# A layer of recurrent heads and pooling on one core: TensorE's side products in one block per slot, the solver's stores on another queue

## The chip, the cores and the metric

The kernel runs on one core of one Trainium2 chip, in one launch. The metric is the device time of an execution in microseconds; the time of a kernel is the median over its runs.

## What is computed

One layer of a decoder: a norm, one input projection of 3200 columns, two kinds of heads that share it, gates, one output projection, the residual and a last norm. There is one prompt of 2048 rows, and eight sequences of four rows each that go on from a given state (the sample).

```python
h = rmsnorm(x); p, g_rwkv, u, g_pool = split(h @ w_in)
ps = p + mu * (previous_row(p) - p);  r, k, v, xw, xa = split(ps)
decay = exp(-exp(-softplus(-(w0 + tanh(xw) @ w_decay)) - 0.5)); a = sigmoid(a0 + xa @ w_aaa)
kk = heads(k * k_k) / norm; k = k * (1 + (a - 1) * k_a)
for t in range(T):                          # per head, S is 64 x 64
    S = S * decay + (S @ -kk) x (kk * a) + v x k;  y[t] = S @ r
o_rwkv = (group_norm(y) + sum(r * k * r_k) * v) * silu(g_rwkv)
o_pool = (windowed_mean(u, 2|4|8|16) - u) @ pool_w * pool_scale * silu(g_pool)
out = rmsnorm(x + concat(o_rwkv, o_pool) @ w_out)
```

The new shift rows, the states S and the last rows of u are outputs too.

## The kernel before

The prompt is worked off in four groups of 512 rows. A group's input projection is 25 column blocks of 128: block 12 (the low-rank inputs) first, then six blocks for each of four pairs of heads: r, k, the pooling input, v, the pooling gate, the heads' gate. Weights and activations are split into a high and a low part of fp32r, so a block is eight **slots** of three matmuls (`pp`, lines 342 to 344: xh with wh, xl with wh, xh with wl), 512 columns wide. The last group also carries the sample and is cut into two runs of 272 columns; there a slot holds six matmuls. `proj` yields after each slot, and `run` (line 458) then calls `side` (line 446).

`side` steps the work that goes beside the projection, one step of each lane and in this order: the lane "solve", then every generator in `late`, then the lanes "prod", "fold" and "chain". What it issues on TensorE gets an edge to the slot's last projection matmul (`tc.issue_after(mark[0])`), so that it stands behind it in TensorE's order. A scheduler then lays out the order of each engine from these edges, the data's dependencies, the order in which the code traced the instructions, and its own model of when inputs are ready. TensorE, like each engine, works its queue off in that order. A pair is 48 slots long. Its side steps on TensorE are:

- `key_norms` (line 499): sums of squares per head (`sq`) eight slots behind the k projection, and the bonus sums (`bo`) six later. It stores the sums to dS in device memory, four small stores issued by ScalarE (line 510).
- `products` (line 572): after three yields, the pair products `pa` (line 585) from abd and bk, one of four blocks per slot. These are what VectorE and ScalarE make of k in `unit` (lines 529 to 548), with line 542 as the last. Then, once the pair before has ended its fold (`pend`), the products `pb` (lines 616 and 617) with two yields between.
- `solve` (line 625): stores the triangle Ab to dA (line 634, issued by ScalarE), loads it back as L in another layout through SP (line 639), waits six yields, and solves in 31 steps on POOL (lines 651 and 653). POOL masks three more tiles (lines 663 and 665), and after YQ = 16 yields TensorE turns the result (`xt`, line 673). Two products (`q1`, line 692, and `q2`, line 700, in one step) finish the inverse.
- `fold` (line 725): for four blocks, `z` (line 730), its copies into zbd, and `f` (line 738), to which VectorE adds the tile F (line 741). One yield lies between these steps.
- `pair_chain` (line 760): eight steps `ch` (line 771), two yields apart, each as soon as the fold has counted its chunk (`folded`). VectorE scales the state (line 773), ScalarE copies the output (line 775).
- `pair_back` (line 800): the group norm of the outputs on VectorE (last instruction line 798), five yields, then the transposes `try` (line 808).
- `values` (line 710, transposes `trv`), `pool_out` (`po`, line 859), `lora_out` (`z` of 512 columns, line 391).

```python
    def run(gen, every):
        for i, _ in enumerate(gen):
            side()
            step("x")
```

The products go into PSUM banks by tag: "pp" three, "mm" two, "pt" two, "ch" one. After the groups, the output projection (`out_tile`, line 1140, three matmuls per slot at lines 1157 to 1160) runs beside the last pairs and the sample. Weights are loaded by ScalarE's queue (lines 311 and 314), in the first group they are split on the way and kept in device memory through SP (line 323).

Of the kernel before, what the change touches and what calls it, by code (L numbers as in the profile page):

```python
# [2 lines left out]

# [13 lines left out]
P = 128  # L17
# [43 lines left out]
def tile_trunk(ctx, tc, xT, xtok, xsT, xstok, par, w_in, wlora, pool_w, w_out, norm_f, st_shift, st_wkv, st_pool,  # L61
               y_p, y_s, nsh_p, nwkv_p, npool_p, nsh_s, nwkv_s, npool_s):
    nc = tc.nc
# [237 lines left out]
    raws, wts, mark = {}, {}, {}  # L301
# [25 lines left out]
    def proj(g, m, xs):  # L327

        i = order.index((g, m))
        hi, lo = wts.pop(i)  # L330
        late_load = i + 2 < len(order) and order[i + 2][0]
        if not late_load:
            w_load(i + 2)
        last = g == NG - 1
        segs = []
        w = 272 if last else 512
        for s in range(2 if last else 1):
            pp = bank("pp", f"pp_{g}_{m}_{s}", 3) if i else bank("ch", "pp_first", 1)
            c = slice(s * w, (s + 1) * w)
            for kc in range(KC):  # L340
                xh, xl = xs[kc]
                PE.matmul(pp[:, :w], hi[:, kc, :], xh[:, c], start=(kc == 0), stop=False)  # L342
                PE.matmul(pp[:, :w], hi[:, kc, :], xl[:, c], start=False, stop=False)  # L343
                mark[0] = PE.matmul(pp[:, :w], lo[:, kc, :], xh[:, c], start=False, stop=(kc == KC - 1)).ins  # L344
                if s == 0 and kc == 2:
                    w_split(i + 1)
                    if late_load:
                        w_load(i + 2)
                if not last or kc % 2:
                    yield  # L350
            if g == 0 and m != 12:
                V.tensor_tensor(out=pp, in0=pp, in1=rb0[0], op=mult)
            if last:
                A.activation(spr[:, m, 16 * s:16 * s + 16], pp[:, 256:272], AF.Copy)
                segs.append((pp, 256 * s, 256))
            else:
                segs.append((pp, 0, G))
        return segs
# [44 lines left out]
            V.scalar_tensor_tensor(out=sg[:, a:a + n], in0=t1[:, a:a + n], scalar=1.0, in1=pp[:, :n], op0=add, op1=mult)  # L403
        return sg

    DH, DZ, DP, YQ = 6, 2, 4, 16

    def c3(ap):
        return ap.rearrange("p (c t) -> p c t", t=CH)
# [3 lines left out]
    rb0, low = [], []  # L413
    pend = [0]
    made = [None]
    chb = []
    lanes = {"prod": [], "solve": [], "fold": [], "chain": [], "x": [], "tail": []}
    late = []
# [23 lines left out]
    def drain(lane):  # L442
        while lanes[lane]:
            step(lane)

    def side():
        if not mark:
            return
        with tc.issue_after(mark[0]):
            step("solve")  # L450

            with tc.high_priority(0):
                step_late()
                step("prod")
                step("fold")
                step("chain")
# [42 lines left out]
    def key_norms(g, j, u, kk2, prod):  # L499

        nm = f"{g}_{j}"
        a = head_sums(kk2, f"sq_{nm}")
        for _ in range(DH + 2):
            yield
        sq = head_sums_mm(a, f"sq_{nm}")
        sqs = sb.tile([P, 512], F32, tag="tmp", name=f"sqs_{nm}", bufs=3)
        A.activation(sqs, sq, AF.Copy)
        for h in range(2):
            for b in range(2):
                nc.scalar.dma_start(u["dS"][b, h:h + 1],  # L510
                                    sqs[64 * h:64 * h + 1].rearrange("p (c b t) -> p b c t", b=2, t=32)[:, b])
        a = head_sums(prod, f"bo_{nm}")
        for _ in range(DH):
            yield
        bo = head_sums_mm(a, f"bo_{nm}")
        u["bv"] = sb.tile([P, 512], F32, tag="bv", name=f"bv_{nm}")
        A.activation(u["bv"], bo, AF.Copy)

    def unit(g, j, xs, nxs, lst, nst):
        nm = f"{g}_{j}"  # L520
        u = {}
        later((DZ if g else DZ + 7) if j == 0 else 1, decay(g, j, lst, u))
        r = shift(g, j, (yield from proj(g, j, xs)), "rps", 1)
        k = shift(g, 4 + j, (yield from proj(g, 4 + j, xs)), "kps", 1)
        while alive[0] >= 2 or lanes["prod"]:
            side()
        alive[0] += 1
        lam, cs, tha = u["lam"], u["cs"], u["tha"]
        kk2 = sb.tile([P, 512], F32, tag="tmp", name=f"kk2_{nm}", bufs=3)
        A.activation(kk2, k, AF.Square, scale=pr[:, KK + j:KK + j + 1])  # L530
        for h in range(2):
            q = slice(64 * h, 64 * h + 64)
            V.scalar_tensor_tensor(out=abd[q, :, q], in0=c3(k)[q], scalar=pr[q, KK + j:KK + j + 1],
                                   in1=lam[q, :, 0:CH], op0=mult, op1=mult)
        ab = sb.tile([P, 512], F32, tag="t1", name=f"ab_{nm}")
        A.activation(ab, tha, AF.Identity, scale=nkk[:, j:j + 1], bias=nkk[:, j:j + 1])
        V.tensor_tensor(out=cs, in0=k, in1=cs, op=mult)
        V.tensor_tensor(out=bk[:, :, 0:CH], in0=c3(cs), in1=c3(ab), op=mult)
        rd = sb.tile([P, NCH, CH], F32, tag="rd", name=f"rd_{nm}", bufs=1)
        V.tensor_tensor(out=rd, in0=c3(r), in1=lam[:, :, 1:], op=mult)  # L540
        A.activation(tha, tha, AF.Identity, scale=hka[:, j:j + 1], bias=oka[:, j:j + 1])
        V.tensor_tensor(out=bk[:, :, CH:2 * CH], in0=c3(cs), in1=c3(tha), op=mult)  # L542
        for h in range(2):
            q = slice(64 * h, 64 * h + 64)
            nc.sync.dma_start(rbd[q, :, h], rd[q])
        prod = sb.tile([P, 512], F32, tag="pd", name=f"prod_{nm}", bufs=1)
        V.scalar_tensor_tensor(out=c3(prod), in0=rd, scalar=pr[:, RK + j:RK + j + 1],
                               in1=bk[:, :, CH:2 * CH], op0=mult, op1=mult)
        dS = dr.tile([2, 2, NCH, 32], F32, tag="dS", name=f"dS_{nm}")
        u.update(rd=rd, dS=dS)  # L550
        lanes["prod"].append(products(g, j, u))
        kn = key_norms(g, j, u, kk2, prod)
        next(kn)
        late.append(kn)
        for m in SEQ[2:]:
            if m == 17:
                d = yield from pool_in(g, j, xs)
            elif m == 8:
                u["v"] = shift(g, 8 + j, (yield from proj(g, 8 + j, xs)), "kps", 1)
                later(8, values(g, j, u))  # L560
            elif m == 21:
                sg = gate(g, 21 + j, (yield from proj(g, 21 + j, xs)), "th0")
                later(DP, pool_out(g, j, d, sg))
            else:
                u["sg"] = gate(g, 13 + j, (yield from proj(g, 13 + j, xs)), "sg")
            if m == (SEQ[3] if SEQ[2] == 8 else 8):
                V.tensor_tensor(out=u["bv"], in0=u["bv"], in1=u["v"], op=mult)
            if m == SEQ[4] and j == NPAIR - 1 and g < NG - 1:
                drain("x")
                lanes["x"].append(prep_x(g + 1, nst, nxs, range(XB - KC, KC)))  # L570

    def products(g, j, u):

        nm = f"{g}_{j}"
        for _ in range(3):
            yield

        ka = sb.tile([P, NCH, P], F32, tag="ka", name=f"ka_{nm}")
# [30 lines left out]
        for b in range(4):  # L609
# [8 lines left out]
            A.activation(f, pb[64:128], AF.Copy)  # L618
            for h in range(2):
                A.activation(rb[64 * h:64 * h + 64, cr, :], pb[0:64, :, h, :], AF.Copy)  # L620
            yield
            yield
        u["made"] = True

    def solve(g, j, u):
# [5 lines left out]
        for h in range(2):  # L631
            for b in range(2):
                o = 64 * h + 32 * b
                nc.scalar.dma_start(dA[b, h].rearrange("c t i -> t c i"), Ab[o:o + 32, :, 32 * b:32 * b + 32])
        L = sb.tile([P, 32, 32], F32, tag="L", name=f"L_{nm}", bufs=1)
        a2 = sb.tile([P, 32], F32, tag="a2", name=f"a2_{nm}")
        for q in range(4):
            nc.sync.dma_start(a2[32 * q:32 * q + 32], dS.rearrange("b h c t -> (b h c) t"))
            nc.sync.dma_start(L[32 * q:32 * q + 32], dA.rearrange("b h c t i -> (b h c) t i"))
        for _ in range(6):  # L640
            yield
        V.tensor_scalar(out=a2, in0=a2, scalar1=L2_EPS, scalar2=None, op0=add)
        V.reciprocal(a2, a2)  # L643
# [39 lines left out]
        with tc.issue_after(made[0]):  # L683
            for h in range(2):
                o = 64 * h + 32
                V.transpose(T22[o:o + 32], tbd[o:o + 32, :, o:o + 32])
        yield
        q1 = [bank("mm", f"q1_{nm}_{h}", 2, (P, NCH, 32)) for h in range(2)]
        for c in range(NCH):
            for h in range(2):  # L690
# [2 lines left out]
        for h in range(2):  # L693
            o = 64 * h
            A.activation(qs[o:o + 32], q1[h][o:o + 32], AF.Copy)
        q2 = [bank("mm", f"q2_{nm}_{h}", 2, (P, NCH, 32)) for h in range(2)]
        for c in range(NCH):
            for h in range(2):
# [26 lines left out]
    def fold(g, j, u):  # L725

        def front(b):
            z = bank("pt", f"z_{g}_{j}_{b}", 2, (P, 2, P))
            for c in range(2):
                PE.matmul(z[:, c, :], tbd[:, 2 * b + c, :], u["rb"][:, 2 * b + c, :], start=True, stop=True)  # L730
            zb = zbd[b % 2]
# [9 lines left out]
            V.tensor_tensor(out=d, in0=f, in1=d, op=add)  # L741
            u["folded"] += 2

        yield
        front(0)
        for b in range(4):
            yield
            if b < 3:
                front(b + 1)
            yield  # L750
            back(b)
        pend[0] = 0
        yield

# [385 lines left out]
    def out_tile(o, res, dst, n, wo, nm):  # L1140
# [12 lines left out]
        for f in range(2):  # L1153
            pp = bank("pp", f"po_{nm}_{f}", 3)
            for c in range(8):
                wh, wl = wo[c, f]
                PE.matmul(pp[:m], hi[:, c, :m], wh, start=(c == 0), stop=False)  # L1157
                mark[0] = PE.matmul(pp[:m], hi[:, c, :m], wl, start=False, stop=(both and c == 7)).ins  # L1158
                if not both:
                    mark[0] = PE.matmul(pp[:n], lo[:, c, :n], wh, start=False, stop=(c == 7)).ins  # L1160
# [123 lines left out]
```

## Time and profile before

| | |
|---|---|
| Median of 3 runs | 1284.83 us (1283.09 to 1289.94) |
| Profiled execution, its own time | 1285.28 us |
| Its span, first to last instruction | 1283.6 us |
| Mean granted TensorE clock | 0.964 of full speed |
| Bytes moved | 200.18 MB, 156 GB/s in the mean |

The profile is one execution. Times are from the start of the span, engines are PE (TensorE matmul), PEld (its weight loads), DVE (VectorE), ACT (ScalarE), POOL (GpSimd) and SP; a name with q behind it is the engine's own instruction queue. A row of a timeline has the start, the duration, the engine, the line, the operation, out<-in by the program's names, shapes and count; in square brackets stands the idle time before it and who ended it. Matmuls overlap, so one matmul's cost to the next is the distance of their starts.

### The profile page before, as it was taken

Reading aid. Unit: us, or ns where it says so; the run is one execution under the profiler, and the core shown is the slowest. Engines: PE = TensorE matmul, PEld = TensorE weight load, DVE = VectorE, ACT = ScalarE, POOL = GpSimd, SP = SyncE. Lnnn points to the kernel's source line nnn. Section 1 sums busy time; section 2 is a strip of 40 time slices with the busy share of each in tenths; the row PEclk is TensorE's granted clock in tenths of the full one; section 3 lists DMA queues with packets and bytes.
Section 4 is the critical chain, followed back from the end, with each engine's and each line's share of the span. In section 5 each row is a group of like instructions: output and inputs, shape, how many; then the busy total and the mean of one; then the engine's idle time right before and its main releaser. Section 6 shows DMA issues by size and latency. Waiting matters only on the chain. (4 is left out here: it accounts for less than half of the span.)

```text
span 1283.6 us, 21090 instructions
## 1 busy us (share of the span) xinstructions
PE 1193.0 (93%) x7229; PEld 982.6 (77%) x7229; DVE 827.3 (64%) x2028; ACT 563.7 (44%) x1363; POOL 503.9 (39%) x1138
## 2 busy tenths in 40 slices
PE   5987989898989999999899899899999999999997
PEld 2766767676878787788688789898889877887685
DVE  5755685957565847766676667565656577745764
ACT  3454545444454544446353546353535453321112
POOL 5045446253252844727164708071808370000000
PEclk6988999999999999999999999999999899999999
DMA  7565655555565544547465546354444354433332
GB/s 246 178 219 177 206 186 178 180 173 156 158 193 164 169 139 152 185 134 200 135 186 160 148 129 188 125 153 138 132 136 136 115 155 155 144 109 99 125 110 69
DMA packets 153372, 200.18 MB, mean 156 GB/s; under 512 B 82480, under 2 KB 99120, under 8 KB 153264
## 3 DMA queue, kind: packets, MB, share of 16 engines
q1 hardware_dynamic: 109632, 104.90, 26.7%
q10 hardware_dynamic: 43632, 93.93, 23.2%
q8 instruction: 57, 0.93, 0.3%
q14 instruction: 51, 0.42, 0.1%
HBM read 139.39 MB, written 46.80 MB: 145 GB/s over the span
## 5 line engine op out<-in xcount | busy, mean ns | idle before, releaser
L342 PE MATMUL pp<-xh,wh 128*128 128x512 f32 (+1 forms) x992 | 367.6, 371 | 7.5 <-ACT xh L204 4.5
L343 PE MATMUL pp<-xl,wh 128*128 128x512 f32 (+1 forms) x992 | 364.7, 368 | 1.4 <-DVE xl L205 1.4
L344 PE MATMUL pp<-xh,wl 128*128 128x512 f32 (+1 forms) x992 | 363.1, 366 | 0.2 <-DVE wl L321 0.2
L342 PEld LDWEIGHTS pp<-xh,wh 128*128 128x128 f32 x992 | 189.9, 192 | 33.7 <-ACT xh L204 5.6
L343 PEld LDWEIGHTS pp<-xl,wh 128*128 128x128 f32 x992 | 189.8, 191 | 25.3 <-DVE xl L205 2.7
L344 PEld LDWEIGHTS pp<-xh,wl 128*128 128x128 f32 x992 | 189.5, 191 | 23.6 <-DVE wl L321 1.7
L651 POOL TENSOR_TENSOR Xt<-X,L 128x60 f32<-128x60 f32 (+24 forms) x496 | 191.9, 387 | 38.8
L653 POOL TENSOR_TENSOR X<-X,Xt 128x60 f32<-128x60 f32 (+24 forms) x496 | 179.8, 363 | 38.9
L646 POOL TENSOR_TENSOR X<-dmask,a 128x256 f32<-128x256 bf16 x16 | 10.8, 676 | 296.1 <-DVE a L643 281.3
L644 POOL TENSOR_TENSOR L<-L,a 128x1024 f32<-128x1024 f32 x16 | 31.1, 1947 | 164.7 <-DMA L<-dA 164.7
L771 PEld LDWEIGHTS ch<-SV,F 128*128 128x128 f32 x512 | 75.2, 191 | 19.7 <-ACT Y L775 8.7
L771 PE MATMUL ch<-SV,F 128*128 128x64 f32 x512 | 79.6, 266 | 3.1 <-ACT Y L775 1.8
L738 PE MATMUL f<-zbd,ka 128*128 128x256 f32 x256 | 68.4, 387 | 0.8 <-DVE zbd L733 0.5
L1157 PE MATMUL po_o<-woh,oh_o 128*128 128x512 f32 x160 | 67.4, 421 | 0.0
L773 DVE TENSOR_TENSOR SV<-ch,lc 64x128 f32<-64x128 f32 x112 | 33.0, 295 | 52.6 <-PE ch L771 47.1
L585 PE MATMUL pa<-bk,abd 128*128 128x192 f32 x256 | 56.2, 366 | 11.0 <-DVE bk L542 9.0
L1158 PE MATMUL po_o<-wol,oh_o 128*128 128x512 f32 x160 | 65.8, 411 | 0.0
L1160 PE MATMUL po_o<-woh,ol_o 128*128 128x512 f32 x160 | 65.1, 407 | 0.1
L733 DVE COPY zbd<-z 64x256 f32<-64x256 f32 x64 | 27.2, 427 | 55.8 <-ACT zbd L732 54.6
L775 ACT ACTIVATE Y<-ch 64x128 f32<-64x128 f32 x128 | 34.3, 268 | 64.3 <-DVE SV L773 56.3
L741 DVE TENSOR_TENSOR F<-f,F 128x512 f32<-128x512 f32 x64 | 44.1, 689 | 27.4 <-PE f L738 24.4
L585 PEld LDWEIGHTS pa<-bk,abd 128*128 128x128 f32 x256 | 49.7, 217 | 15.8 <-DVE bk L542 7.0
(447 smaller groups left out, 2332.7 us busy)
## 6 DMA issues: line engine op xcount, KB each, us to landing
wh<-wh ACTq DMA_DIRECT2D x75, 512.0 KB
wl<-wl ACTq DMA_DIRECT2D x75, 512.0 KB
wr<-in_w_in ACTq DMA_DIRECT2D x25, 512.0 KB
wh<-wh SPq DMA_DIRECT2D x25, 512.0 KB
wl<-wl SPq DMA_DIRECT2D x25, 512.0 KB
xr<-in_xT SPq DMA_DIRECT2D x32, 256.0 KB
L<-dA SPq DMA_DIRECT2D x64, 128.0 KB
oi<-o_d SPq DMA_DIRECT2D x16, 512.0 KB
```

The source lines that it names most:

```text
L342: PE.matmul(pp[:, :w], hi[:, kc, :], xh[:, c], start=(kc == 0), stop=False)
L343: PE.matmul(pp[:, :w], hi[:, kc, :], xl[:, c], start=False, stop=False)
L344: mark[0] = PE.matmul(pp[:, :w], lo[:, kc, :], xh[:, c], start=False, stop=(kc == KC - 1)).ins
L585: PE.matmul(pa[:, c, :], abd[:, 2 * b + c, :], bk[:, 2 * b + c, :], start=True, stop=True)
L651: GP.tensor_tensor(out=tm, in0=X[:, :n, i:i + 1].broadcast_to([P, n, w]), in1=L[:, i + 1:, i].unsqueeze(1).broadcast_to([P, n, w]), op=mult)
L653: done = GP.tensor_tensor(out=X[:, :n, i + 1:], in0=X[:, :n, i + 1:], in1=tm, op=add).ins
L738: PE.matmul(f[:, c].rearrange("p h t -> p (h t)"), u["ka"][:, 2 * b + c, :], zbd[b % 2][:, c].rearrange("p h t -> p (h t)"), start=True, s ...
L741: V.tensor_tensor(out=d, in0=f, in1=d, op=add)
L771: PE.matmul(ch[:, h, :], fm[cc // 4][:, cc % 4, h, :], sv[cc // 4][:, cc % 4, h, :], start=True, stop=True)
L1157: PE.matmul(pp[:m], hi[:, c, :m], wh, start=(c == 0), stop=False)
L1158: mark[0] = PE.matmul(pp[:m], hi[:, c, :m], wl, start=False, stop=(both and c == 7)).ins
L1160: mark[0] = PE.matmul(pp[:n], lo[:, c, :n], wh, start=False, stop=(c == 7)).ins
```

## The change

TensorE's order gets a second edge. `side` keeps the last TensorE instruction that its steps traced (`lastpe`), and the next slot's first matmul is issued behind it (`behind`). The yields between the side steps change: three to six ahead of `pa`, two to three between the `pb` blocks, six to eight in `solve`, YQ from 16 to 9, one more ahead of `q1`, two between `q1` and `q2`, one more ahead of the first `z`; within the fold one more ahead of each `f` and two behind it, so that a block of the fold takes five slots instead of two; eight to twelve ahead of `values`. `z` takes its bank from tag "mm" instead of "pt". The stores of dS and dA are issued by SP instead of ScalarE. The arithmetic is the same.

```diff
@@ proj
-                PE.matmul(pp[:, :w], hi[:, kc, :], xh[:, c], start=(kc == 0), stop=False)
+                with behind():
+                    PE.matmul(pp[:, :w], hi[:, kc, :], xh[:, c], start=(kc == 0), stop=False)
@@
-    DH, DZ, DP, YQ = 6, 2, 4, 16
+    DH, DZ, DP, YQ = 6, 2, 4, 9
+    lastpe = []
+    def behind():
+        return tc.issue_after(lastpe.pop()) if lastpe else nullcontext()
     def side():
         if not mark:
             return
+        block = nc.cur_bb.bb.instructions
+        at = len(block)
+        side_steps()
+        pe = [i for i in block[at:] if i.engine == mark[0].engine]
+        if pe:
+            lastpe[:] = pe[-1:]
+
+    def side_steps():
         with tc.issue_after(mark[0]):
             step("solve")
@@ key_norms
-                nc.scalar.dma_start(u["dS"][b, h:h + 1],
+                nc.sync.dma_start(u["dS"][b, h:h + 1],
@@ unit
-                later(8, values(g, j, u))
+                later(12, values(g, j, u))
@@ products
-        for _ in range(3):
+        for _ in range(6):
             yield
...
-            yield
-            yield
+            for _ in range(3):
+                yield
         u["made"] = True
@@ solve
-                nc.scalar.dma_start(dA[b, h].rearrange("c t i -> t c i"), Ab[o:o + 32, :, 32 * b:32 * b + 32])
+                nc.sync.dma_start(dA[b, h].rearrange("c t i -> t c i"), Ab[o:o + 32, :, 32 * b:32 * b + 32])
...
-        for _ in range(6):
+        for _ in range(8):
             yield
...
-        yield
+        for _ in range(2):
+            yield
         q1 = [bank("mm", f"q1_{nm}_{h}", 2, (P, NCH, 32)) for h in range(2)]
...
+        for _ in range(2):
+            yield
         q2 = [bank("mm", f"q2_{nm}_{h}", 2, (P, NCH, 32)) for h in range(2)]
@@ fold
-            z = bank("pt", f"z_{g}_{j}_{b}", 2, (P, 2, P))
+            z = bank("mm", f"z_{g}_{j}_{b}", 2, (P, 2, P))
...
-        yield
+        for _ in range(2):
+            yield
         front(0)
         for b in range(4):
             yield
             if b < 3:
                 front(b + 1)
             yield
+            yield
             back(b)
+            yield
+            yield
         pend[0] = 0
         yield
@@ out_tile
-                PE.matmul(pp[:m], hi[:, c, :m], wh, start=(c == 0), stop=False)
+                with behind():
+                    PE.matmul(pp[:m], hi[:, c, :m], wh, start=(c == 0), stop=False)
```

## Rows read from the trace of the kernel before

**Rows 1.** The page, first part: busy time, share of the span, instructions.

```profile
PE 1193.0 (93%) x7229; PEld 982.6 (77%) x7229; DVE 827.3 (64%) x2028; ACT 563.7 (44%) x1363; POOL 503.9 (39%) x1138
```

**Rows 2.** Busy time by stretch: start:end, length, then each engine, clock, DMA.

```profile
60.00:1284.00 1224.00, 1149.46 (x7083) 954.15 (x7081) 790.28 (x1960) 539.27 (x1326) 484.85 (x1085) 0.97 0.50 153
```

**Rows 3.** Waits of TensorE: who waited for whom, total us, times, longest.

```profile
PE try L808 <- DVE Y L798: 14.2, 13, 3.2
PE pa L585 <- DVE bk L542: 9.0, 3, 3.3
PE sq L476 <- ACT h_sq L469: 8.2, 3, 3.4
PE xt L673 <- POOL X L653: 7.6, 1, 7.6
...
PE try L808 <- DVE carry L372: 4.2, 1, 4.2
```

**Rows 4.** Timeline of TensorE, 628 to 658 us.

```profile
628.86 0.40 PE L344 MATMUL pp<-xh,wl 128*128 128x512 f32 x1
629.09 0.39 PE L342 MATMUL pp<-xh,wh 128*128 128x512 f32 x1
...
657.22 0.48 PE L344 MATMUL pp<-xh,wl 128*128 128x512 f32 x1
657.54 0.40 PE L391 MATMUL z<-sw,lwh 128*128 128x512 f32 x1
```

**Rows 5.** Timeline, all engines, 641 to 645 us: one product of the fold.

```profile
641.45 1.08 PE L738 MATMUL f<-zbd,ka 128*128 128x256 f32 x4
...
642.18 0.58 PE L342 MATMUL pp<-xh,wh 128*128 128x512 f32 x1
...
642.60 0.39 PE L343 MATMUL pp<-xl,wh 128*128 128x512 f32 x1
...
642.63 0.69 DVE L741 TENSOR_TENSOR F<-f,F 128x512 f32<-128x512 f32 x1 [1.29 <-PE f L738]
...
643.38 0.43 PE L771 MATMUL ch<-SV,F 128*128 128x64 f32 x2
```

**Rows 6.** Line 741, duration ns min/median/max, and who waited for it.

```profile
L741 DVE TENSOR_TENSOR F<-f,F x64: 672/691/693, 133.4 to 1092.9; 128x512 f32<-128x512 f32 x64
...
  PEld z L730: 4.2, 7
```

**Rows 7.** Timelines of ScalarE, VectorE and TensorE, 607 to 618 us: a pair's start.

```profile
607.38 0.69 ACT L367 ACTIVATE t<-pp,om 128x512 f32<-128x512 f32 x1 [0.83 <-PE pp L344]
...
616.70 0.68 DVE L542 TENSOR_TENSOR bk<-cs,th 128x512 f32<-128x512 f32 x1
...
616.76 0.50 PE L476 MATMUL sq<-h_sq,bonr 128*128 128x512 f32 x1 [3.39 <-ACT h_sq L469]
...
617.53 0.98 PE L585 MATMUL pa<-bk,abd 128*128 128x192 f32 x2
```

**Rows 8.** Timelines of TensorE and VectorE, 593 to 604 us: a pair's end.

```profile
593.20 0.56 PE L771 MATMUL ch<-SV,F 128*128 128x64 f32 x4
...
602.86 0.69 DVE L798 TENSOR_TENSOR Y<-Y,st 128x512 f32<-128x512 f32 x1
...
603.70 0.63 PE L808 MATMUL try<-ident,Y 128*128 128x128 f32 x4 [0.85 <-DVE Y L798]
```

**Rows 9.** Line 634, the stores of dA: duration of one issue, ns.

```profile
L634 ACTq DMA_DIRECT2D dA<-Ab x64: 309/326/980, 70.0 to 1009.2; - x64
```

**Rows 10.** Waits of SP's queue, columns as in rows 3.

```profile
SPq L639 <- DMA dA<-Ab: 107.0, 28, 11.0
```

**Rows 11.** Timelines of POOL and TensorE, 609 to 631 us: solver's end, its transposes.

```profile
612.30 1.28 POOL L665 TENSOR_TENSOR rb<-rb,mkr 128x512 f32<-128x512 f32 x1
...
629.55 0.60 PE L673 MATMUL xt<-ident,X 128*32 128x128 f32 x4
```

**Rows 12.** Busy time by stretch, columns as in rows 2.

```profile
617.30:620.60 3.30, 3.30 (x10) 3.06 (x10) 2.38 (x6) 0.90 (x3) 0.00 (x0) 0.50 0.40 144
```

More of the change, by code (lines that the diff above doesn't have):

```diff
@@ L1 @@
 import math
-from contextlib import ExitStack
+from contextlib import ExitStack, nullcontext
 import concourse.bass as bass
```

## The prediction

> **What bounds the kernel now.** The first view is the page's first part: TensorE is busy for 93% of the span, and no other engine for more than 64% [rows 1]. The table by stretches says how much is left to win: after the first 60 us TensorE is busy 1149.5 of 1224 us, so it waits for 74.5 us in all [rows 2]. The list of TensorE's waits names them: the transposes of the normed outputs (try) behind VectorE, 14.2 and 4.2 us; the first pair products (pa) behind bk, 9.0; the key norms (sq) behind h_sq, 8.2; the transposes of the solved blocks (xt) behind POOL, 7.6 us, once [rows 3]. So the kernel is TensorE's work in a row. Whatever the change does reaches the end by making TensorE wait, or by sparing it work, and other engines count only where TensorE waits for them.
>
> One slot is three matmuls of 512 columns, each 0.23 us behind the one before (628.86, 629.09 [rows 4]): 0.70 us. In the last group a slot is six narrower ones and much the same.
>
> **The change, part by part.** Today only the lower side is tied: a side product comes behind its slot's last projection matmul, but the next slots' matmuls may pass it. I read this off the trace: they do, wherever an input is late. The change ties the other side as well: the next slot's first matmul comes behind the last side product that the slot traced. A product that waits now holds all of TensorE.
>
> *Fold and chain.* The fold's back matmul (f) and the chain's next step (ch) are traced in the same slot, in this order, and the chain reads what VectorE's add (line 741) makes of f. Four times per pair this holds in the new code too: back raises the count of folded chunks, and the chain lane, stepped right behind, goes on at once. Today the gap is filled: f starts at 641.45, a projection matmul follows at 642.18, the add runs from 642.63 for 0.69 us, ch starts at 643.38, and from 642.18 to 643.38 TensorE does four projection matmuls [rows 5]. With the change it does nothing there: 1.20 us, less 0.19 that the first of the four loses (0.42 us to its successor instead of 0.23), so 1.0 us. There are 64 such adds, all of 0.67 to 0.69 us [rows 6], so 64 us. What can still slip in is the next projection: its first slots hang on no side product if the slot before traced none. Counting the new yields through a pair, that is one slot behind the chain's sixth step and two behind its last: 2.1 us of the pair's 4.0. But what is used here is missing as cover at try. Least 16 x 1.9 = 30 us; most 64 x 1.2 = 77 us, with 0.2 more for adds that start late because VectorE is at something else (my estimate); I take one of the four covered, **+48 us**.
>
> *Pair products.* The three yields ahead of pa become six, so pa stands seven slots behind the k projection. In the trace the scheduler put it later than the code has it: in one pair the shift of k starts at 607.38, 26 projection matmuls follow (8.7 slots), bk is done at 617.38 (616.70 + 0.68), and TensorE still waited 3.39 us, at sq; pa starts at 617.53 [rows 7]. Counted alike, pa stands 8 to 14 slots behind in the twelve pairs of groups 1 to 3, 10 in the mean. Seven slots are three fewer, 2.1 us of cover: all of it is lost in a pair that waits already, part of it where bk was early. I take half, 16 x 1.05 = **+16 us**; none if VectorE gets to k sooner, 34 if all is lost.
>
> *Normed outputs.* The five yields ahead of try stay, the passing goes. The last chain step runs at 593.20, the last norm operation ends at 603.55 (602.86 + 0.69) and try starts at 603.70, having waited 0.85 us [rows 8]: 10 us from step to product. In the new code try stands eight slots behind the last step, with three of the next pair's four pb blocks among them: 8 x 0.70 = 5.6 us, and some 0.8 us for each pb (my estimate, from f's four matmuls, 0.73 us between 641.45 and 642.18 [rows 5], and a change of kind), 8.0 us. That is 2 us short in this pair and, as it is one of the longer ones, perhaps 1.4 in the mean: 16 x 1.4 = 22 against 18.4 today [rows 3], **+4 us**; between -18 (all goes) and +40.
>
> *Changes of kind.* Behind a side product the projection matmul is slow: ch at 657.08, matmul at 657.22, the next start at 657.54, 0.32 us against 0.23 [rows 4]. So 0.09 us for each block, and the 64 chain blocks that join their fold's block save 64 x 0.09 = **-6 us**; from 0, if other blocks split, to -12, if as many again join. [...]
>
> *The rest.* z moves to the mm banks: the waits of z's weight loads for the fold's add, 4.2 us of which little reached TensorE [rows 6], can go, and z may meet xt or po instead: **-1 us**, from -4 to +3. The stores of dA and dS, 128 issues of about 0.33 us each [rows 9], leave ScalarE, whose 44% hide them, for SP, where they stand ahead of the loads of L and a2. Those wait on SP for these very stores already (107 us [rows 10]), so nothing useful is queued behind a new wait; what else SP holds (rbd, F, x) is needed many slots later. The solver gets its input some microseconds sooner: 0. It needs that, since xt moves up: nine slots instead of sixteen behind the masks. In the pair shown POOL ends its last mask at 613.58, and xt starts at 629.55 [rows 11], so 16 us stand between; seven slots with their side work take some 9 of them: 0 as well, unless POOL becomes late in single pairs. The wait of 7.6 us in the first pair stays. The longer pauses between the pb blocks let their lane run past the unit's start in seven units, by 13 rounds without projection behind them; they hold pb blocks that have to run anyway: 0.
>
> **Sum:** 48 + 16 + 4 - 6 - 1 = +61 on the profiled execution's 1285.28 us, 1346.3. That execution stands 0.45 us above the median of the runs shown, so **1346 us**.
>
> **The rivals.** *Faster.* The place is the boundary of a pair and the fold. If the free first slots of the next projections cover all four gaps of the fold (it decides whether at least 1 us lies free at each, and the count above finds two places per pair), and the even spread gives VectorE the time for bk and the norm, so that half of the 45 us of waits at try, pa, sq and xt [rows 3] go, the time is 1285 - 22 - 6 = 1257. For it: pa, trv and pb do move towards where the trace has them. Against: try and the chain do not move. 18%.
>
> *Hardly any change.* The fold's gaps are filled as before and the boundaries keep their waits; only the 6 us go, and small new waits eat them: about 1283. It also holds if the tie is not kept in the issue order. 9%.
>
> *Slower still.* [...] 10%.
>
> **How the numbers follow.** The forecast has 63%, with a range of its own from 1305 to 1385 out of the bounds of the terms. A measurement of this kernel tells about 0.5% (6.4 us) from no change. Faster: 0.18. Same: 0.09. Slower: 0.63 + 0.10 = 0.73. The range has to reach into the faster case: 1262 to 1390 leaves out about half of it and most of the case slower still, some 18% together.
>
> **What would show it.** Right: in TensorE's waits ch behind the add with 64 entries near 1 us, pa or sq behind bk in most pairs, and in the timeline no projection matmul between f and the ch of its slot. The count of f, ch and pp matmuls stays. Wrong: projection matmuls of another projection standing between f and ch; TensorE's idle time after 60 us below 75 us; the solver's xt waiting in many pairs, which would mean that the seven slots were not spare.

## The result, and the profile after

The changed kernel takes 1374.86 us in the median of four runs (1370.02 to 1378.26), the one before 1283.96 us beside it: a ratio of 1.0683, with an interval of 1.0644 to 1.0722. The profiled execution of the changed kernel has a span of 1374.5 us, 90.9 us more than before, and a mean granted clock of 0.945 instead of 0.964.

The first part of the page answers to [rows 1]:

```profile
span 1374.5 us, 21213 instructions
PE 1209.1 (88%) x7229; PEld 987.7 (72%) x7229; DVE 812.0 (59%) x2028; ACT 566.4 (41%) x1363; POOL 458.6 (33%) x1138
```

The number of TensorE instructions is the same. Its busy time rose by 16.1 us, its share fell from 93% to 88%, and no other engine came near to being the bound. The table by stretches, from 60 us to the end, answers to [rows 2]:

```profile
60.00:1374.50 1314.50, 1170.35 (x7103) 963.37 (x7103) 774.90 (x1962) 542.15 (x1326) 439.41 (x1085) 0.95 0.47 143
```

TensorE now waits 1314.50 - 1170.35 = 144.2 us of this stretch; before it was 1223.6 - 1149.46 = 74.1 us (up to the end of its span). So 70 us of the 91 are new waiting, and 21 us are matmuls that lasted longer or overlapped less. TensorE's list of waits (us in total, times, longest) answers to [rows 3]:

```profile
PE ch L792 <- DVE F L758: 50.5, 49, 2.9
PE pa L599 <- DVE bk L556: 22.0, 11, 6.7
PE z L392 <- DVE sw L384: 14.1, 4, 5.5
PE try L829 <- DVE Y L819: 9.8, 8, 2.3
PE xt L687 <- POOL X L667: 8.8, 1, 8.8
...
PE pa L599 <- DVE ka L601: 6.1, 4, 1.8
```

The chain's step behind the add, which is not among the waits of [rows 3], leads with 50.5 us in 49 waits. One of them in the timeline, beside [rows 5]:

```profile
703.26 1.02 PE L755 MATMUL f<-zbd,ka 128*128 128x256 f32 x4
...
704.39 0.69 DVE L758 TENSOR_TENSOR F<-f,F 128x512 f32<-128x512 f32 x1
...
705.13 0.66 PE L792 MATMUL ch<-SV,F 128*128 128x64 f32 x4 [0.85 <-DVE F L758]
```

Between f and ch stands no projection matmul in this block; TensorE is through with f, VectorE adds for 0.69 us, and only then ch goes on. In another block of the same pair the gap is filled:

```profile
718.62 1.03 PE L755 MATMUL f<-zbd,ka 128*128 128x256 f32 x4
...
719.30 0.59 PE L345 MATMUL pp<-xh,wl 128*128 128x512 f32 x1
...
719.73 0.40 PE L343 MATMUL pp<-xh,wh 128*128 128x512 f32 x1
...
720.55 0.63 PE L792 MATMUL ch<-SV,F 128*128 128x64 f32 x4
```

Here matmuls that hang on no side product slip in, and ch waits for nothing. In 49 of the 64 blocks ch waited for the add, in 15 it did not (two of these stood idle for 0.9 us all the same, which the list has under other names). Counted from the order of the matmuls, 43 blocks have no projection matmul between f and ch and 21 have some, 13 of these at the third block of a pair; in a few of the 21 ch waits all the same.

New in the list is z of line 392, the low-rank product, which waits for VectorE in the first pair of each group, 14.1 us in four waits (0.5, 5.5, 5.4 and 2.6 us). try's wait fell, from 18.4 us [rows 3] to 9.8. The two belong together: three of the waits of z stand between a pair's last chain step and its try, here one in the timeline of TensorE:

```profile
592.64 0.55 PE L792 MATMUL ch<-SV,F 128*128 128x64 f32 x4
...
602.07 0.79 PE L392 MATMUL z<-sw,lwh 128*128 128x512 f32 x1 [5.43 <-DVE sw L384]
...
607.40 0.60 PE L829 MATMUL try<-ident,Y 128*128 128x128 f32 x4
```

While TensorE stood for z, VectorE's last norm operation (line 819) ran, from 598.80 for 0.69 us, and try started 7.9 us behind its end.

The granted clock behind a wait is shown by three stretches of 4 us from the end of a wait on, in the table by stretches (the last columns are the granted clock, the DMA share and GB/s):

```profile
705.13:709.13 4.00, 4.00 (x23) 3.52 (x24) 0.94 (x4) 0.72 (x3) 3.13 (x12) 1.00 0.14 56
582.20:586.20 4.00, 4.00 (x14) 3.52 (x15) 0.93 (x3) 1.14 (x3) 3.22 (x11) 0.50 0.23 52
602.07:606.07 4.00, 4.00 (x11) 3.20 (x12) 1.65 (x2) 0.99 (x2) 0.00 (x0) 0.57 0.00 0
```

Behind the wait of 0.85 us shown above the granted clock is 1.00; behind a wait of ch of 2.87 us it is 0.50, as in [rows 12] behind the wait of 3.39 us at sq, and 14 matmuls run where 23 did; behind a wait of z for 5.43 us it is 0.57. The clock's records of the two executions hold 1.00 and 0.50 alone, and 153.4 us of them are at 0.50, against 94.9 us before.

### The profile page after: what moved, and what is told of

Its sections match the earlier page's. It is cut to its first block, busy times and chain, and to the rows that moved or that the text cites. A ratio compares the mean times of both kernels' runs of the same rounds, so it can differ in the third digit from the quotient of the medians.

```text
span 1374.5 us, 21213 instructions
## 1 busy us (share of the span) xinstructions
PE 1209.1 (88%) x7229; PEld 987.7 (72%) x7229; DVE 812.0 (59%) x2028; ACT 566.4 (41%) x1363; POOL 458.6 (33%) x1138
## 4 chain that ended last, share of the span: by engine, by line
PE 63%; DVE 18%; ACT 6%; DMA 5%; issue 4%; POOL 3%; SPq 1%; ACTq 0%; DVEq 0%; POOLq 0%
PE pp L343 10%; PE pp L344 9%; PE pp L345 9%; PE ch L792 4%; PE po_o L1179 4%; PE po_o L1182 4%; PE po_o L1180 4%; PE pa L599 3%; PE f L755 3%; DVE F L758 2%; PE z L747 2%; DMA xr<-in_xT 2%; DMA xt_g<-in_xtok 2%; DVE abd L547 1%; POOL X L667 1%
## 5 line engine op out<-in xcount | busy, mean ns | idle before, releaser
L343 PE MATMUL pp<-xh,wh 128*128 128x512 f32 (+1 forms) x992 | 395.4, 399 | 3.9 <-ACT xh L204 3.5
L344 PE MATMUL pp<-xl,wh 128*128 128x512 f32 (+1 forms) x992 | 357.4, 360 | 1.0 <-DVE xl L205 1.0
L345 PE MATMUL pp<-xh,wl 128*128 128x512 f32 (+1 forms) x992 | 358.1, 362 | 0.0
L343 PEld LDWEIGHTS pp<-xh,wh 128*128 128x128 f32 x992 | 193.3, 195 | 23.9 <-ACT xh L204 4.7
L344 PEld LDWEIGHTS pp<-xl,wh 128*128 128x128 f32 x992 | 193.7, 195 | 19.2 <-DVE xl L205 1.8
L665 POOL TENSOR_TENSOR Xt<-X,L 128x60 f32<-128x60 f32 (+24 forms) x496 | 170.6, 344 | 38.8
L667 POOL TENSOR_TENSOR X<-X,Xt 128x60 f32<-128x60 f32 (+24 forms) x496 | 159.8, 322 | 38.9
L792 PE MATMUL ch<-SV,F 128*128 128x64 f32 x512 | 80.4, 281 | 56.3 <-DVE F L758 50.5
L677 POOL TENSOR_TENSOR F<-F,mkr 64x512 f32<-64x512 f32 x32 | 43.8, 1369 | 174.2 <-ACT F L632 157.2
L599 PE MATMUL pa<-bk,abd 128*128 128x192 f32 x256 | 58.7, 353 | 28.1 <-DVE bk L556 22.0
L599 PEld LDWEIGHTS pa<-bk,abd 128*128 128x128 f32 x256 | 45.7, 203 | 38.2 <-issue 21.6
L755 PEld LDWEIGHTS f<-zbd,ka 128*128 128x128 f32 x256 | 48.4, 193 | 9.8 <-issue 1.2
```

The source lines that it names most:

```text
L599: PE.matmul(pa[:, c, :], abd[:, 2 * b + c, :], bk[:, 2 * b + c, :], start=True, stop=True)
L665: GP.tensor_tensor(out=tm, in0=X[:, :n, i:i + 1].broadcast_to([P, n, w]), in1=L[:, i + 1:, i].unsqueeze(1).broadcast_to([P, n, w]), op=mult)
L667: done = GP.tensor_tensor(out=X[:, :n, i + 1:], in0=X[:, :n, i + 1:], in1=tm, op=add).ins
L755: PE.matmul(f[:, c].rearrange("p h t -> p (h t)"), u["ka"][:, 2 * b + c, :], zbd[b % 2][:, c].rearrange("p h t -> p (h t)"), start=True, s ...
L792: PE.matmul(ch[:, h, :], fm[cc // 4][:, cc % 4, h, :], sv[cc // 4][:, cc % 4, h, :], start=True, stop=True)
```

## The experiments

The theory after the result: the edge itself is the loss. A product that waits holds all of TensorE, mostly at the fold, and the new yields only set how late its input is. The rivals: the yields, the bank of z or the stores through SP cost the time, or only the fold's order within a slot does. All ratios are to the kernel before on the same chip; its median there was 1286.59 us for the first four runs, 1284.74 for the next four, 1284.64 for the last four. In the tables, us is the median and clock the mean granted clock of the profiled execution.

**The parts of the change**

*e1_chain_first.* The chain steps ahead of the fold, so that one slot lies between f and the ch that needs it.

```diff
                 step("prod")
-                step("fold")
                 step("chain")
+                step("fold")
```

> The changed kernel with the chain's lane stepped ahead of the fold's, so that a chain step reads what VectorE made of a product of an earlier slot. Theory (a product that reads, through VectorE, another of its own block stops TensorE for the add): the 50.5 us of waits of ch for the add go, with some of the low clock behind them; 1300 to 1330 us, and below 10 us of waits of ch for the add. Rival (TensorE held to a fixed order always waits somewhere, and the wait only moves to the next product): above 1350 us, with the waits of f, z and pa grown by as much as those of ch shrank.

*e2_order_free.* All new yields, the bank and the queue stay, the second edge goes.

```diff
-        return tc.issue_after(lastpe.pop()) if lastpe else nullcontext()
+        return nullcontext()
```

> The changed kernel without its new edge: the next slot's first matmul is free again, all new yields, the z bank and the SP stores stay. Theory (the edge makes the waits): within 1 per cent of the kernel before, 1272 to 1297 us. Rival (the wider spacing of the side products or the stores on SP cost by themselves): above 1310 us.

*e3_sp_only.* The kernel before with the stores of dS and dA on SP, nothing else.

```diff
-                nc.scalar.dma_start(u["dS"][b, h:h + 1],
+                nc.sync.dma_start(u["dS"][b, h:h + 1],
...
-                nc.scalar.dma_start(dA[b, h].rearrange("c t i -> t c i"), Ab[o:o + 32, :, 32 * b:32 * b + 32])
+                nc.sync.dma_start(dA[b, h].rearrange("c t i -> t c i"), Ab[o:o + 32, :, 32 * b:32 * b + 32])
```

> The kernel before with the stores of dS and dA issued by SP alone. Theory (no engine on the path waits for them): 1279 to 1291 us, no change. Rival (a store waiting at the head of SP's queue holds the loads behind it, or the solver's earlier input spares TensorE a wait): more than 6 us away from the kernel before, to either side.

*e4_tie_only.* The kernel before with the second edge, nothing else: the old yields, bank and queue.

```diff
-                PE.matmul(pp[:, :w], hi[:, kc, :], xh[:, c], start=(kc == 0), stop=False)
+                with behind():
+                    PE.matmul(pp[:, :w], hi[:, kc, :], xh[:, c], start=(kc == 0), stop=False)
```

> The kernel before with the new edge alone, at the old yields, bank and store queue. With the old yields only one chain step in a pair reads a product of its own slot, but q2 reads q1 of its own slot, pa stands three slots nearer to the k projection and the transposes of v four slots nearer to theirs. Theory (each product that is traced before its input is ready stops TensorE): 1385 to 1430 us, with waits of pa above 45 us, of ch for the add near 16, of q2 near 13. Rival (the loss comes from the new yields, and the edge alone costs little): below 1350 us.

| | us | ratio | interval | clock |
|---|---|---|---|---|
| e1_chain_first | 1358.13 | 1.0566 | 1.0525 to 1.0607 | 0.948 |
| e2_order_free | 1269.62 | 0.9882 | 0.984 to 0.9924 | 0.965 |
| e3_sp_only | 1284.26 | 0.9984 | 0.9956 to 1.0011 | 0.961 |
| e4_tie_only | 1458.02 | 1.1332 | 1.1268 to 1.1396 | 0.923 |

The edge on the new yields costs 1374.86 - 1269.62 = 105 us, and on the old ones 1458.02 - 1286.59 = 171 us. The new yields, with the bank and the queue, gain 1.2%. SP's stores make no difference that can be measured. The waits of e4 show what the new yields are good for once the order is tied:

```profile
PE pa L599 <- DVE bk L556: 58.1, 13, 6.9
PE try L822 <- DVE Y L812: 41.8, 12, 8.9
PE pa L599 <- DVE nwt_g L55: 15.8, 2, 10.0
PE ch L785 <- DVE F L755: 14.7, 16, 2.0
```

With the old yields pa waits for 73.9 us and try for 41.8, where the changed kernel has 28.1 and 9.8, while ch waits far less. e4 was slower than I had expected (1385 to 1430).

e1 fell short of what I had expected as well (1300 to 1330): putting the fold's pair right gives 17 us, not 50. The timeline and the waits of e1:

```profile
695.49 1.02 PE L755 MATMUL f<-zbd,ka 128*128 128x256 f32 x4
696.16 0.58 PE L343 MATMUL pp<-xh,wh 128*128 128x512 f32 x1
...
697.36 0.66 PE L792 MATMUL ch<-SV,F 128*128 128x64 f32 x4 [0.16 <-DVE F L758]
```

```profile
PE pa L599 <- DVE bk L556: 33.5, 12, 6.7
PE ch L792 <- DVE F L758: 16.0, 35, 2.2
PE try L829 <- DVE Y L819: 12.8, 8, 2.4
...
PE try L829 <- DVE rs_g L57: 4.2, 2, 2.2
```

The fold did what was wanted (50.5 to 16.0 us), but pa went from 22.0 to 33.5 and try from 9.8 to 17.0 in the two lines shown. One reading is that while TensorE stood at the fold, VectorE came on with bk and the norm, so that with this standing gone part of it is stood out at the next late product. That is not shown: in e6 below the waits of ch are gone too, and pa for bk and try for the norm together grow by only 3 us.

**The terms of the loss**

*e6_chain_untied.* The chain's step comes behind the slot's other side work, outside of what the next slot waits for.

```diff
         side_steps()
         pe = [i for i in block[at:] if i.engine == mark[0].engine]
+        with tc.issue_after(mark[0]), tc.high_priority(0):
+            step("chain")
...
-                step("chain")
```

> The changed kernel with the chain's steps left out of the new edge, all other side products kept in it. Theory (waits add up: the 50.5 us at ch and the low clock behind them are a term of their own): 1305 to 1330 us. Rival (pa and try wait for a run of VectorE work that takes its time whatever TensorE does, so that a wait taken away at the chain is largely waited there): 1335 to 1362 us, as with the chain stepped first, and waits at pa and try 10 us or more above the changed kernel's 38 us.

*e7_chain_alone.* The opposite: only the chain's step gives the edge, all other side products may be passed.

```diff
-        at = len(block)
         side_steps()
+        at = len(block)
+        with tc.issue_after(mark[0]), tc.high_priority(0):
+            step("chain")
         pe = [i for i in block[at:] if i.engine == mark[0].engine]
...
-                step("chain")
```

> The changed kernel with the chain's steps alone in the new edge. Theory (waits add up): the 1270 us of the kernel without the edge, and 64 gaps of about 0.8 to 1.1 us: 1318 to 1345 us. Rival (the wait at the chain is cover for pa and try, so that it costs only a part): below 1310 us.

*e5_all_later.* The tie stays, and every late product gets more slots: the chain first, the fold's count one yield later, pa behind nine yields, the key norms' sums (and the bonus sums behind them) two later, the low-rank products four later, try behind nine; YQ goes down to 6.

```diff
-    DH, DZ, DP, YQ = 6, 2, 4, 9
+    DH, DZ, DP, YQ = 6, 6, 4, 6
...
-                step("fold")
                 step("chain")
+                step("fold")
...
-        for _ in range(DH + 2):
+        for _ in range(DH + 4):
...
-        for _ in range(6):
+        for _ in range(9):
...
-            u["folded"] += 2
...
             yield
+            u["folded"] += 2
             yield
...
-        for _ in range(5):
+        for _ in range(9):
```

> The changed kernel, edge kept, with every side product that waited moved to a later slot: a chain step two slots behind the fold's product that it reads, pa and sq three and two slots later, the low-rank products of a group's first pair four, the transposes of the normed outputs four; three yields fewer behind the masks. Theory (the edge only shows which products are traced before their inputs are ready; late enough, they cost nothing): 1270 to 1305 us, waits of ch, pa, try and the low-rank z together below 25 us. Rival (readiness varies with VectorE's queue from pair to pair, and no fixed slot fits them all, or the wait moves on with each gain): above 1320 us, those waits still above 45 us.

*e8_free_yq12.* e2 (no tie) with the solver's xt four yields later.

```diff
-    DH, DZ, DP, YQ = 6, 2, 4, 9
+    DH, DZ, DP, YQ = 6, 2, 4, 13
```

> The changed kernel without its new edge and with 13 instead of 9 yields behind the solver's masks. Without the edge xt waited for POOL twice, 16.7 us together. Theory: the second wait of 5 us or more goes, 1257 to 1268 us. Rival (the wait in the second pair is cover for what follows and comes back, or the later fold costs as much): 1269 us or more.

| | us | ratio | interval | clock |
|---|---|---|---|---|
| e5_all_later | 1293.38 | 1.007 | 1.0036 to 1.0104 | 0.959 |
| e6_chain_untied | 1319.89 | 1.0265 | 1.0198 to 1.0333 | 0.957 |
| e7_chain_alone | 1305.90 | 1.0174 | 1.0119 to 1.0228 | 0.966 |
| e8_free_yq12 | 1289.96 | 1.0036 | 1.0009 to 1.0063 | 0.963 |

e6 takes 55 us off the changed kernel, what its ch waits came to and some more, and leaves the other terms near where they were (pa for bk from 22.0 to 27.9, try from 9.8 to 6.6). By the table from 60 us on, TensorE waits 1256.80 - 1155.07 = 101.7 us, 42 us less than in the changed kernel, and is busy for 15 us less:

```profile
60.00:1316.80 1256.80, 1155.07 (x7103) 953.79 (x7103) 781.77 (x1962) 542.18 (x1326) 453.26 (x1085) 0.96 0.48 150
```

```profile
PE pa L600 <- DVE bk L557: 27.9, 11, 6.7
PE z L392 <- DVE sw L384: 13.9, 4, 5.4
...
PE try L830 <- DVE Y L820: 6.6, 7, 2.2
```

e7 adds 36 us to e2, less than I had expected (1318 to 1345), in the band that I had given the rival:

```profile
PE ch L793 <- DVE F L759: 24.3, 28, 2.0
```

28 blocks waited here instead of 49. With everything else free to move, more of the fold's gaps are filled. So the two halves, 36 us for the chain alone and 1319.89 - 1269.62 = 50 us for all others alone, come to 86 us, and the whole edge costs 105: tied together they cost 19 us more than apart. The theory's "mostly at the fold" is not borne out: the chain is worth 36 us alone and 55 us on top of the others, so from a third to a half of the edge.

e5 wins back 81 of the 91 us by delays alone. What is left stands at q1 (15.4 us for X of line 700), xt and ch:

```profile
PE q L707 <- DVE X L700: 15.4, 10, 4.2
PE xt L687 <- POOL X L667: 15.1, 4, 10.0
PE ch L792 <- DVE F L758: 9.6, 9, 3.3
PE xt L687 <- ACT tbd L691: 7.2, 2, 3.6
```

e8 was slower than I had expected (1257 to 1268). It shows that later is not better by itself: without any tie, four yields more cost 20 us against e2. xt no longer leads the waits, and the waits stand at try (20.9 us), pa (18.6) and sq (8.4) instead:

```profile
PE try L829 <- DVE Y L819: 20.9, 13, 2.1
PE pa L599 <- DVE bk L556: 18.6, 12, 2.2
PE sq L490 <- ACT h_sq L483: 8.4, 4, 2.5
```

**Is the tie worth anything once the sites are late enough?**

*e9_later_yq9.* e5 with YQ back at 9.

```diff
-    DH, DZ, DP, YQ = 6, 6, 4, 6
+    DH, DZ, DP, YQ = 6, 6, 4, 9
```

> The kernel with all waiting products later, the edge kept, and 9 instead of 6 yields behind the solver's masks. It waited 22 us at xt and 15 us at q1 for POOL and VectorE. Theory (each wait is a term of its own): most of the 12 us of xt beyond the first pair go and part of those at q1, 1270 to 1285 us. Rival (three slots later the pair's end meets the next pair's start, as in the free kernel with 13 yields): 1290 us or more, with try and pa waiting over 20 us together.

*e10_later_yq9_free.* e9 without the second edge.

```diff
-        return tc.issue_after(lastpe.pop()) if lastpe else nullcontext()
+        return nullcontext()
```

> The same without the edge. Theory (the edge, once all products come late enough, neither costs nor gives): within 10 us of the run with the edge. Rival (blocks spare changes of kind, some 0.09 us for each of about 250): 15 us or more slower than with the edge; or (the free order still passes single late products): 15 us or more faster.

*e11_free_old_bank.* e2 with z back in its old bank.

```diff
-            z = bank("mm", f"z_{g}_{j}_{b}", 2, (P, 2, P))
+            z = bank("pt", f"z_{g}_{j}_{b}", 2, (P, 2, P))
```

> The changed kernel without its new edge and with z back in its old banks. Theory (the gain of the kernel without the edge over the kernel before comes from the new yields): 1264 to 1276 us. Rival (it comes from f and z no longer sharing two banks): 1280 us or more, with waits of z behind the fold's add.

*e12_later_q1.* e5 with three more yields ahead of q1, where its largest wait was.

```diff
-        for _ in range(2):
+        for _ in range(5):
             yield
         q1 = [bank("mm", f"q1_{nm}_{h}", 2, (P, NCH, 32)) for h in range(2)]
```

> The kernel with all waiting products later, the edge kept, and q1 three slots further from the turned blocks it reads. Theory (each wait is a term of its own): the 15 us at q1 go, 1275 to 1287 us. Rival (VectorE turns the blocks late in any case, or the wait moves on to ch, try or pa): 1290 us or more.

| | us | ratio | interval | clock |
|---|---|---|---|---|
| e9_later_yq9 | 1278.41 | 0.9958 | 0.9933 to 0.9982 | 0.962 |
| e10_later_yq9_free | **1234.81** | 0.9613 | 0.9569 to 0.9658 | 0.971 |
| e11_free_old_bank | 1272.77 | 0.99 | 0.9864 to 0.9937 | 0.965 |
| e12_later_q1 | 1285.85 | 1.0013 | 0.9987 to 1.0039 | 0.954 |

The tied e9 is 0.4% faster than the kernel before; without the edge the same yields give 3.9%, which is the second rival of e10. e10 beats both kernels of the case. Which of its delays brings the 2.7% over e2 was not run one by one. The two in the table by stretches, e9 and then e10:

```profile
60.00:1272.90 1212.90, 1135.77 (x7094) 949.45 (x7094) 780.80 (x1960) 539.72 (x1324) 457.56 (x1085) 0.97 0.50 155
```

```profile
60.00:1234.90 1174.90, 1127.26 (x7082) 938.73 (x7080) 783.86 (x1960) 537.56 (x1325) 472.17 (x1085) 0.98 0.51 159
```

The tie costs 77.1 - 47.6 = 29.5 us of waiting and 8.5 us more of busy time, though the sites are the same. What the tie was to spare, changes from side products to the projection, does not pay for it: counted from the matmuls' starts, an fp32 product followed by an fp32r one, there are about 446 in e9 and 706 in e10, and e10 is busy for less. The leading waits of e9, then of e10:

```profile
PE pa L599 <- DVE ka L601: 13.4, 12, 2.6
PE xt L687 <- POOL X L667: 9.1, 1, 9.1
```

```profile
PE xt L687 <- POOL X L667: 11.3, 2, 10.1
...
PE sq L490 <- ACT tbd L691: 6.7, 4, 2.8
```

The products that came late in e9 are passed in e10: pa waits 0.7 us there for ka. The longest wait that is left is the solver's, 10.1 us once, in the first pair.

e11 differs from e2 by 3 us, within both intervals: the bank is worth nothing that can be measured. e12 removes the wait of q1 that e5 had, but the gain is 1293.38 - 1285.85 = 7.5 us where 15.4 had stood there, and between the two profiled executions only 2.8 us; pa, which waited 0.3 us in e5, now waits 15.9 us for ka: a wait that moved on.

## Why the prediction was right, and where it was off

**The mechanism and the sign** came out as forecast: the second edge turns late products into idle time, TensorE's idle time after 60 us went to 144 us and not below 75, and xt did not wait in many pairs (8.8 us, once). 1346 us was 29 us short of the median, inside the range.

**Fold and chain, +48 us:** right in mechanism and size. The ch waits came to 50.5 us, 1.03 us each, with 15 of 64 blocks without one; the forecast took 1.0 us and one in four. Part of this is luck: 33 of the waits last 0.85 to 0.88 us, less than was taken, and eight of 1.8 to 2.9 us, where the add came late, make 18.6 of the 50.5. Projection matmuls between f and ch, named as a sign of being wrong, stand in 21 blocks, against the 16 that the sum allowed. Taking the term away from the changed kernel gives 55 us (e6), putting it alone on e2 36 us (e7): its size hangs on what else is tied.

**Pair products, +16 us:** the right sign. pa and sq together stood at 9.0 + 8.2 + 1.8 = 19.0 us before and at 28.1 us after, +9 us. The sum had taken half of the lost cover. e1 and e4 show why such a term has no fixed size: pa waited 33.5 + 5.2 = 38.7 us with the chain first, and 73.9 us with the old yields.

**Normed outputs, +4 us:** the wrong sign, though inside its bounds. try's waits fell by 8.6 us. The step that failed is the one that put a mean shortfall of 1.4 us on all 16 pairs. At the end of three pairs (try at 340.45, 607.40 and 872.61) try started 8.4, 7.9 and 7.0 us behind the norm's end, and of this TensorE stood for the low-rank z, between the last chain step and try, for 5.5, 5.4 and 2.6 us: time that is paid at z. What the rest of it comes from is open. The other 13 pairs waited 0.75 us each in the mean.

**Changes of kind, -6 us:** the blocks joined as forecast, in direction: about 404 changes against 428 before. At 0.09 us each that is 2 us, a part of the term. By e9 and e10 the number of changes is not what decides.

**The bank, SP's stores: about nothing,** as e11 and e3 show one by one. The 0.33 us for one issue is right for dA [rows 9] alone: the 64 stores of dS took ScalarE 0.61 us each in the median (line 510).

**What was missing** is more than the 29 us. First the low-rank z, 14.1 us: the prediction's walk through the side products began at pa and never came to the first pair of a group, where z is two slots behind the split of its input on VectorE (line 384) and was passed until then. It should have asked the same question of each product that the tie holds. e2 has 1.4 us at this place and e5, with four yields more there, has no wait for line 384 among its largest. Second the clock: the sum priced every wait by its own length. The records have 153.4 - 94.9 = 58.5 us more at 0.50 than before. In the changed kernel the projection's matmuls start 0.43 us apart at 0.50 (583.62 and 584.05 us) and 0.23 us apart at 1.00 (578.48, 578.70 and 578.94 us), so about half of such time is lost: by this estimate 29 us at most, as some of it was idle anyway; busy time rose by 21 us. The case slower still was held at 10%; the time stayed inside the forecast's own range, with part of its loss at a clock of 0.50.

**The sum again, with what was measured:** waits of ch +50, pa and sq +9, z +14, try -9, xt +1, and some 5 us in single waits of ch, z and others give the 70 us of idle time; with the 21 us of busy time that is the 91 us of the spans. So z and the longer matmuls, 35 us, had no term, and the terms of pa and try were 20 us too large. That these partly cancel, and 1346 comes as near as it does, is luck.

## What to carry to other kernels

Before TensorE's order is fixed as it was here, list every product that it will hold and compare, one by one, when its input is ready with when its slot comes: one left out, here the low-rank z with 14.1 us, is not small because the rest was counted with care. Delays that give inputs time and an order that may not be passed are two changes; here the delays, taken further, were worth 3.9% without the tie and 0.4% with it. The length of a wait is not what its removal gives back: it was less in e1 (17 us of 34.5) and e12 (some 7.5 of 15.4), where other waits grew, and more in e6 (55 us for 48), where busy time fell as well.

## What was not expected of the hardware

Waits of about a microsecond did not cost the clock in these kernels, even in numbers: e7 has 24.3 us more waiting at ch than e2, in 28 waits, and its clock is 0.966 against 0.965. Each wait of the changed kernel after its first 60 us, with the granted clock of the 4 us behind it taken as in the rows of stretches above: of 37 waits of 0.8 to 1.2 us that began at the full clock, one was followed by less than 0.9; of 17 waits of 2 us and more, all were. In e7 it was three of seven such waits. e4, with waits of up to 10 us, has the lowest mean clock of all, 0.923. So the length of the wait alone does not say it, and what else of TensorE's work does was not tried and stays open.

What a change between an fp32 side product and the projection costs in the end is not settled. Some 260 more of them in e10 than in e9, at the 0.09 us of [rows 4] each, would be 23 us, and e10's busy time is 8.5 us lower instead. That does not show that they cost less: at the full clock the first 512-column matmul behind a side product stands 0.32 us ahead of its successor in the median of e9 and of e10 alike. Busy time holds other things besides: e10 has 33 waits after 60 us and e9 has 70, each behind a matmul whose whole duration counts because no other overlaps its end (0.40 us at 578.94 us of the changed kernel, where the next start comes 0.23 us on when one follows), and e10's clock records have 74.1 us at 0.50 against 98.4, at mean clocks of 0.971 and 0.962. These runs do not tell the shares apart.
